# All gates of a five-branch encoder in the seven-product scheme, their sum in DRAM

## The chip, the cores and the metric

The kernel runs on one core of one Trainium2 chip. Times are device microseconds (us) of that core, from start to end of one execution; less is better. Engines: PE is TensorE, DVE is VectorE, ACT is ScalarE, POOL is GpSimd, and SP issues DMAs.

## What is computed (the reference, cut)

Two layers. In each, `h` is the normalised input of 1024 tokens by 1024 channels, five branches of 256 channels are computed from it, and each is projected to 1024 channels, gated and summed:

```python
for l in range(DEPTH):                                   # DEPTH = 2
    h = rmsnorm(x, norm_pre[l])
    (..., ca, cb, cz, ...) = split_cols(h @ w_in[l])
    y_cf = conformer_branch(ca, cb, cz, ...)             # and y_hg, y_sc, y_at, y_mem
    for n, yb in enumerate((y_hg, y_cf, y_sc, y_at, y_mem)):
        term = jax.nn.sigmoid(h @ w_gate[l, n]) * (yb @ w_branch[l, n])
        merged = term if merged is None else merged + term
    x = x + rmsnorm(merged @ w_out[l], norm_post[l])

def conformer_branch(a, b, z, ...):
    u = a * sigmoid(b)
    c = depthwise_conv(u, w_dw) + b_dw                   # 31 taps along the tokens
    mu = mean(c, channels); var = mean(square(c - mu), channels)
    n = (c - mu) * rsqrt(var + EPS) * ln_g + ln_b
    return silu(n) * silu(z)
```

## The kernel before, in words

Channels lie on the 128 partitions and tokens along the free axis, in halves of 512. Every fp32 product is made of three matmuls on values split into a high and a low part (`hi` made by a cast on ACT, `lo` by a subtraction on DVE), so a 128 x 128 weight block against 512 tokens is three matmuls of 128 x 512.

**Who sets the order.** `drive` (L465) runs a list of items, each a product with what is done to its result, and prepares the next item's weights while one runs. Work that is not a product (the convolution, attention, the forms below) is written as generators handed to `plan.side`; a planner with a small cost model puts pieces of them between the items. The order on each engine is thus fixed when the program is built, and every instruction carries the line of the planner's wrapper, L116.

**The gates.** `h @ w_gate` is five products of 1024 x 1024 per layer. Two forms exist. `gate_item` (L1137) is the plain one: 48 matmuls for 128 output channels. `strassen_items` (L1217) takes 256 output channels at a time, called a group, by seven products P1 to P7 of 12 matmuls instead of eight, 84 matmuls instead of 96. Their order is P1, P6, P5, P2, P7, P3, P4. P1 and P2 go to the PSUM bank `ps_gX`, P5 and P3 to `ps_gZ`, and P6, P7 and P4 to `ps_gY`. So P4 starts on `ps_gY` only when DVE has read P7's sum from it (`g_u<-ps_gY`, the `u3` of the code), and P7 only when DVE has read P6's. Beside it DVE adds and splits weight blocks (`g_s`, `raw_g`, `lo`) for products to come. The right-hand sides T1 to T4 are sums of blocks of `h`, made by `gate_forms` (L1175) on DVE: 32 additions `b<-h,h` that put high and low part together, further ones, and the splits.

**Before the change**, in each layer, branch 2 (eight items), the first quarter of branch 0 (two items) and the conformer's output gate `cz` (two items, `use_z`, L684) are plain; the other 15 groups are in the seven-product form, channel group by channel group, and each gated term is added by DVE to a running sum `mg` in SBUF (`merge`, L1261). The convolution and LayerNorm of the conformer (`conv`, L623) run on DVE and ACT beside the branch products (`ps_b`, 96 matmuls per branch) and the plain gates; two short matmul pairs, `cf_mu` and `cf_var`, make the means. The forms follow them.

Of the kernel before, what the change touches and what calls it, by code (L numbers as in the profile page):

```python
# [14 lines left out]
AF = mybir.ActivationFunctionType  # L15
# [5 lines left out]
P = 128  # L21
# [54 lines left out]
class Meter:  # L76
# [5 lines left out]
    def __getattr__(self, name):  # L82
        f = getattr(self.engine, name)

        def call(*args, **kw):
# [6 lines left out]
            if self.key == "PE":  # L92
                split = name != "transpose" and kw["rhs"].dtype == F32R
                if name == "transpose":
                    cost = 0.107
                elif split:
                    cost = 0.0135 + 0.000418 * n
                else:
                    tiled = outs[0].shape[0] <= HD or kw["lhsT"].shape[0] <= HD
                    cost = max(0.212, 0.00167 * n) * (0.7 if tiled else 1.0)  # L100
                cost += 0.09 * (split != self.plan.split)
                self.plan.split = split
            elif self.key == "DVE":
                n = max([n] + [prod(x.shape[1:]) for x in tiles])
                each = {"reciprocal": 0.0063, "tensor_scalar": 0.0005, "tensor_copy": 0.0006}.get(name, 0.00107)
                fixed = {"scalar_tensor_tensor": 0.16, "tensor_scalar": 0.23, "copy_predicated": 0.12}.get(name, 0.07)
                cost = fixed + n * each + 0.1 * ("accum_out" in kw)
            elif self.key == "ACT":
                cost = 0.055 + n * 0.00087 + 0.22 * ("accum_out" in kw) + self.plan.table(kw.get("func"))
            elif self.key == "DMA":  # L110
# [10 lines left out]
class Planner:  # L121


    def __init__(self):
        self.t = dict.fromkeys(("PE", "DVE", "ACT", "POOL", "DMA"), 0.0)
        self.written, self.read = {}, {}
        self.last = 0.0
        self.flags = set()
        self.sides = []
        self.rings = {}  # L130
        self.loaded = None
        self.split = True

    def add(self, key, cost, outs, ins):
# [3 lines left out]
        for x in outs:  # L138
            t = max([t] + [v for k, v in self.read.get(x, {}).items() if k != key])
        if key == "DMA":  # L140
            t = max(t, self.t["PE"])
        end = t + cost
        self.t[key] = end
        seen = end + (2.0 if key == "DMA" else 0.2)
        for x in outs:
# [66 lines left out]
def encoder(ctx: ExitStack, tc: tile.TileContext, a: dict, out: bass.AP):  # L212
# [5 lines left out]
    pool = Meter(nc.gpsimd, "POOL", plan)  # L218
    load = Meter(nc.sync, "DMA", plan).dma_start
    x_in = a["x"][0]  # L220
    mem_in = a["mem"][0]
# [389 lines left out]
    def conformer_items(l, hT, cs):  # L611
# [11 lines left out]
        def conv():  # L623
            yield f"merge{l}"
            for j in range(2):
                yield f"cf_u{l}{j}"
                u = us[j]
                c = cs[j] = slot(f"cf_c{j}")
                mid = CONFK // 2
                dve.tensor_scalar(out=c, in0=u, scalar1=wt[:, j, mid:mid + 1], scalar2=vec[:, j, 0:1],  # L630
                                  op0=ALU.mult, op1=ALU.add)
                for k in range(CONFK):
                    if k == mid:
                        continue
                    o = k - mid
                    dst = c[:, max(0, -o):T - max(0, o)]
                    src = u[:, max(0, o):T - max(0, -o)]
                    dve.scalar_tensor_tensor(out=dst, in0=src, scalar=wt[:, j, k:k + 1], in1=dst,
                                             op0=ALU.mult, op1=ALU.add)
                    if k % 2:  # L640
                        yield
            for s in range(2):
# [164 lines left out]
    def memory_attention_items(l, hT, kv, zs):  # L807
        qs = [None] * NH
        ks = []

        def stack_keys():
            for v in range(2):
                ks.append(slot(f"m_k{v}", F32R).rearrange("p (h m) -> p h m", h=NH))
                for h in range(NH):
                    rows = slice((h % 2) * HD, (h % 2 + 1) * HD)
                    for part in range(2):
                        act.copy(out=ks[v][part * HD:(part + 1) * HD, h, :],
                                 in_=kv["k"][rows, part ^ v, h // 2, :].bitcast(F32))

        items = []  # L820
        for j in range(2):
            def use_q(s, ps, j=j):
                if s == 0 and j == 0:
                    stack_keys()
                for hh in range(2):
# [6 lines left out]
        sc = HD ** -0.5  # L832

        def worker(j, par):
            yield f"m_in{l}{j}"
            for b in range(par, NT, 2):
# [35 lines left out]

        def workers():
            for j in range(2):
                for par in range(2):
# [299 lines left out]
    def gate_forms(l, hT, forms):  # L1175
# [15 lines left out]

        yield f"cf{l}"
        for i in range(2):
            if i:
                yield f"plain{l}"
            dst = {}
            for k in range(2):
                b11, b12, b22, b21 = (h2(f"b{x}") for x in range(4))
                for b, K, s in ((b12, 0, 1), (b11, 0, 0), (b22, 1, 1), (b21, 1, 0)):
                    hi, lo = (hT[s][v][2 * K + i][:, k, :].bitcast(F32) for v in range(2))  # L1200
                    dve.tensor_tensor(out=b, in0=hi, in1=lo, op=ALU.add)
                yield
                dve.tensor_tensor(out=b11, in0=b12, in1=b11, op=ALU.subtract)
# [13 lines left out]
    def strassen_items(l, groups, forms, pbd, mg, mgd, mT):  # L1217


        order = ("P1", "P6", "P5", "P2", "P7", "P3", "P4")  # L1220
        right = {"P1": "B11", "P2": "B21", "P3": "B22", "P4": "T4", "P5": "T1", "P6": "T2", "P7": "T3"}
# [4 lines left out]
        def load_group(gi):  # L1226
            n, g = groups[gi]
            wg = a["w_gate"][l, n].rearrange("(k p) c -> p k c", p=P)
            raws[gi] = []
            for d in (2 * g, 2 * g + 1):  # L1230
                raw = wp.tile([P, KC, P], F32, tag="raw", bufs=4, name=f"raw_g{n}{d}")
                load(out=raw, in_=wg[:, :, d * P:(d + 1) * P])
                raws[gi].append(raw)
# [48 lines left out]
        def after(k):  # L1282
            gi, name = k // N, order[k % N]
            n, g = groups[gi]
            b = banks[gi]
            if name == "P1":
                b["E1"] = h2("g_e1")
                act.copy(out=b["E1"], in_=b["X"])
                flush()
                if g not in mg:  # L1290
                    mg[g] = []
# [4 lines left out]
                pbs[gi] = []  # L1296
                for dd in range(2):
                    pbs[gi].append(slot("pb"))
# [26 lines left out]
            if gi == len(groups) - 1:  # L1325
                if name in ("P1", "P6", "P5"):
# [15 lines left out]
        for k in range(N * len(groups)):  # L1342
# [26 lines left out]

            need = f"forms{l}" if k == 1 else None  # L1370
            items.append(Item(prep, body, need))
# [60 lines left out]
    with tc.manual_schedule(engines={mybir.EngineType.PE, mybir.EngineType.DVE, mybir.EngineType.Activation,  # L1432
# [30 lines left out]
        def program():  # L1463
# [22 lines left out]
            for l in range(NL):  # L1486
# [8 lines left out]
                else:  # L1495
# [12 lines left out]
                mg = {0: [None, None]}  # L1508
                sc_g = [gate_item(l, 2, d, hT, pbd[2], mg[0], mgd[d // 2] if d > 1 else None, True)
                        for d in range(KC)]  # L1510
                hg_g = [gate_item(l, 0, d, hT, pbd[0], mg[0], None, False) for d in range(2)]
# [4 lines left out]
                cz[1].flag = f"plain{l}"  # L1516
                sc_b = branch_items(l, 2, y_sc, pbd[2])
                sc_b[0].flag = f"merge{l}"
                yield from sc_b
# [49 lines left out]
```

## Time and profile before

| What | Value |
|---|---|
| three runs | 2289.66, 2289.63, 2287.46 us; median 2289.63 |
| the profiled execution | 2287.26 us, of which the span shown is 2285.5 us |
| granted clock of PE, mean | 0.997 of full speed |
| busy in the span | PE 98%, PEld (weight loads) 81%, DVE 70%, ACT 43%, POOL 1% |
| stage of the 15 seven-product groups, layer 0 | 773.1 to 1058.7 us |
| the chain that ended last | PE 89%, DVE 7%, ACT 3% |

The busy share of PE counts its matmuls, not its waits; which waits end last in a stage is read from the timeline of that stage. Names in the trace are the program's without buffer numbers.

### The profile page before, as it was taken

To read this page: it belongs to the slowest core of one execution; us is meant where nothing else is said; L and a number is where in the kernel's file an instruction comes from. 1 tells how busy PE (TensorE), PEld (TensorE's weight loads), DVE (VectorE), ACT (ScalarE), POOL (GpSimd) and SP (SyncE) were. 2 spreads that over 40 slices of the span, in tenths; PEclk is the share of its full clock that TensorE was granted. 3 is DMA by queue.
4 is the path that set the end of the run, shared out by engine and by line. 5 is a ranking of instruction groups with operands and counts; after the bars stand their busy time and mean duration, and the time that the engine had idled before them with its cause. 6 is when DMAs were issued, how large, how long until landed. Compare 5 with 4: busy or idle time off the path is not lost.

```text
span 2285.5 us, 30510 instructions
## 1 busy us (share of the span) xinstructions
PE 2244.6 (98%) x11560; PEld 1841.1 (81%) x11560; DVE 1601.1 (70%) x2798; ACT 974.3 (43%) x1948; POOL 28.5 (1%) x41
## 2 busy tenths in 40 slices
PE   7999999999999999999999999999999999999998
PEld 6886788888888888887887878888788888888876
DVE  6768745347978688887667686363588696888865
ACT  5342435355435533335452423453453454333342
POOL 1000000000000000000110000000000000000000
PEclk9999999999999999999999999999999999999999
DMA  6102121103542633345440101211045535333244
GB/s 204 48 15 74 29 54 45 38 19 132 192 152 97 212 129 129 111 129 185 164 122 29 38 29 37 37 46 46 33 165 176 161 102 194 129 129 114 96 150 166
DMA packets 248019, 237.35 MB, mean 104 GB/s; under 512 B 29984, under 2 KB 191008, under 8 KB 247872
## 3 DMA queue, kind: packets, MB, share of 16 engines
q1 hardware_dynamic: 247872, 235.40, 31.7%
q8 instruction: 91, 1.49, 0.3%
q14 instruction: 56, 0.46, 0.1%
HBM read 177.69 MB, written 57.67 MB: 103 GB/s over the span
## 4 chain that ended last, share of the span: by engine, by line
PE 89%; DVE 7%; ACT 3%; issue 1%; DMA 0%; SPq 0%; POOL 0%; DVEq 0%; ACTq 0%; POOLq 0%
PE ps_gY L116 10%; PE ps_b L116 10%; PE ps_g L116 10%; PE ps_gX L116 7%; PE ps_o L116 7%; PE ps_gZ L116 7%; PE ps_hf L116 4%; PE h_s L116 2%; PE ps_cb L116 2%; PE ps_ca L116 2%; PE ps_at_z L116 2%; PE ps_hq L116 2%; PE ps_sz L116 2%; PE ps_cz L116 2%; PE ps_hz L116 2%; PE ps_sc L116 2%
## 5 line engine op out<-in xcount | busy, mean ns | idle before, releaser
L116 DVE TENSOR_TENSOR lo<-raw_g,hi 128x512 fp32r<-128x512 f32 x220 | 149.6, 688 | 91.7 <-ACT hi L116 91.5
L116 DVE SCALAR_TENSOR_TENSOR cf_c<-cf_u,cfw,cf_c 128x1009 f32<-128x1009 f32 (+14 forms) x120 | 153.1, 1276 | 3.0
L116 ACT CAST hi<-raw_g 128x512 fp32r<-128x512 f32 x220 | 133.4, 616 | 49.2 <-PE ps_gY L116 46.3
L116 PE MATMUL ps_b<-yh,hi 128*128 128x512 f32 x320 | 126.9, 397 | 0.0
L116 PE MATMUL ps_b<-yh,lo 128*128 128x512 f32 x320 | 124.7, 390 | 0.0
L116 PE MATMUL ps_b<-yl,hi 128*128 128x512 f32 x320 | 124.7, 390 | 0.0
L116 ACT COPY pb_out<-ps_b 128x512 f32<-128x512 f32 x160 | 91.7, 591 | 71.4 <-PE ps_b L116 59.6
L116 DVE TENSOR_TENSOR lo<-raw_in,hi 128x512 fp32r<-128x512 f32 x120 | 77.3, 686 | 40.6 <-ACT hi L116 40.4
L116 ACT ACTIVATE g_e<-g_e 128x512 f32<-128x512 f32 x60 | 38.0, 634 | 134.8 <-DVE g_e L116 134.8
L116 PE MATMUL ps_gX<-h_0h,hi 128*128 128x512 f32 x240 | 93.4, 389 | 0.0
L116 PE MATMUL ps_gX<-h_0h,lo 128*128 128x512 f32 x240 | 93.4, 389 | 0.0
L116 PE MATMUL ps_gX<-h_0l,hi 128*128 128x512 f32 x240 | 93.4, 389 | 0.0
L116 ACT CAST hi<-raw_in 128x512 fp32r<-128x512 f32 x120 | 69.2, 621 | 44.9 <-issue 18.7
L116 PEld LDWEIGHTS h_s<-hQQ,hkp 64*128 64x128 f32 x896 | 60.0, 187 | 21.7 <-issue 14.3
L116 PE MATMUL h_s<-hQQ,hkp 64*128 64x128 f32 x896 | 72.6, 294 | 2.8 <-ACT hkp L116 2.0
L116 DVE TENSOR_TENSOR lo<-raw_wo,hi 128x512 fp32r<-128x512 f32 x64 | 42.2, 688 | 47.2 <-PE ps_o L116 29.9
L116 DVE COPY_PREDICATED hS<-masks,h_s 128x512 f32<-128x512 uint8 x112 | 75.2, 726 | 0.0
L116 PEld LDWEIGHTS ps_b<-yh,hi 128*128 128x128 f32 x320 | 60.1, 188 | 13.3 <-issue 2.1
L116 PEld LDWEIGHTS ps_b<-yl,hi 128*128 128x128 f32 x320 | 60.1, 188 | 12.7
L116 ACT COPY hkp<-hK 128x512 f32<-128x512 f32 x56 | 37.3, 665 | 77.3 <-DVE hK L116 77.3
L116 PEld LDWEIGHTS ps_b<-yh,lo 128*128 128x128 f32 x320 | 60.2, 188 | 11.2
L116 ACT CAST hi<-raw_wo 128x512 fp32r<-128x512 f32 x64 | 37.8, 620 | 60.0 <-PE ps_o L116 47.0
(555 smaller groups left out, 6483.5 us busy)
## 6 DMA issues: line engine op xcount, KB each, us to landing
raw_g<-in_w_gate_dram SPq DMA_DIRECT2D x80, 512.0 KB, 3.5
pb<-pb_out SPq DMA_DIRECT2D x160, 256.0 KB, 2.5
pb<-pb SPq DMA_DIRECT2D x80, 512.0 KB, 4.6
raw_in<-in_w_in_dram SPq DMA_DIRECT2D x68, 512.0 KB, 3.7
raw_wo<-in_w_out_dram SPq DMA_DIRECT2D x32, 512.0 KB, 4.7
raw_b<-in_w_branch_dram SPq DMA_DIRECT2D x20, 512.0 KB, 4.9
mg<-g_th SPq DMA_DIRECT2D x24, 256.0 KB, 2.1
mg<-mg SPq DMA_DIRECT2D x12, 512.0 KB, 5.7
```

The source lines that it names most:

```text
L116: return f(*args, **kw)
```

## The change

1. All 20 gate groups of a layer take the seven-product form, branch by branch: `round1` has branches 2, 0, 3 and 4, and after the fifth branch product follow the four groups of branch 1. `gate_item` is no longer called. A seventeenth group in `round1`, named `z`, at index 15, computes `cz` in the same form.
2. In `round1` DVE only multiplies gate and branch (`merge`). Branch 2's terms are stored to DRAM (`mgd`) by SP; those of 0, 3 and 4 are added there by accumulating DMAs that POOL issues, 48 per layer. Branch 1's groups load that sum and go on as before.
3. In `gate_forms` the `b` additions become a copy DMA of the high part (SP) and an accumulating DMA of the low part (POOL), 16 per layer.
4. The convolution is split in token halves (240 instructions of up to 512 columns in place of 120 of about 1,015), waits for the flag `at{l}` instead of `merge{l}`, and its LayerNorm falls into the groups of `round1`. The memory branch's items stand earlier in the list, and its keys are stacked by a side generator on ACT.

Over both layers PE has 144 matmuls of 128 x 512 less: 960 of plain gates and 192 of `cz` go, and 12 groups of 84 come.

```diff
         def conv():
-            yield f"merge{l}"
+            yield f"at{l}"
...
-                dve.tensor_scalar(out=c, in0=u, scalar1=wt[:, j, mid:mid + 1], scalar2=vec[:, j, 0:1],
-                                  op0=ALU.mult, op1=ALU.add)
+                for s in range(2):
+                    dve.tensor_scalar(out=c[:, hs(s)], in0=u[:, hs(s)], ...)
+                yield
...
+                    for s in range(2):
+                        a, b = max(s * HALF, -o), min((s + 1) * HALF, T - max(0, o))
+                        dst, src = c[:, a:b], u[:, a + o:b + o]
+                        dve.scalar_tensor_tensor(out=dst, in0=src, scalar=wt[:, j, k:k + 1], in1=dst,
+                                                 op0=ALU.mult, op1=ALU.add)
+                    yield
...
                     hi, lo = (hT[s][v][2 * K + i][:, k, :].bitcast(F32) for v in range(2))
-                    dve.tensor_tensor(out=b, in0=hi, in1=lo, op=ALU.add)
-                yield
+                    load(out=b, in_=hi)
+                    accumulate(out=b, in_=lo)
+                yield f"plain{l}" if i else None
...
         def merge(gi, dd, s, th):
             n, g = groups[gi]
-            m, pb = mg[g][s][:, dd, :], pbs[gi][dd]
+            pb = pbs[gi][dd]
             dve.scalar_tensor_tensor(out=th, in0=th, scalar=1.0, in1=pb[:, hs(s)], op0=ALU.add, op1=ALU.mult)
-            dve.tensor_tensor(out=m, in0=m, in1=th, op=ALU.add)
+            if mT is not None:
+                m = mg[g][s][:, dd, :]
+                dve.tensor_tensor(out=m, in0=m, in1=th, op=ALU.add)
+            elif n == 2:
+                load(out=mgd[g][s][:, dd, :], in_=th)
+            else:
+                accumulate(out=mgd[g][s][:, dd, :], in_=th)
...
-                yield from cf
...
-                yield from hz + mem
...
-                yield from sc_g[:1] + branch_items(l, 0, o_hg, pbd[0]) + sc_g[1:3] + at_b + sc_g[3:] + hg_g
-                yield from cz + mem_b + branch_items(l, 1, y_cf, pbd[1])
-                groups = [(n, g) for g in range(4) for n in ((3, 4, 1) if g == 0 else (0, 3, 4, 1))]
-                yield from strassen_items(l, groups, forms, pbd, mg, mgd, mT)
+                hg_b = branch_items(l, 0, o_hg, pbd[0])
+                at_b[1].flag = f"plain{l}"
+                yield from mem[:2] + cf[:2] + mem[2:] + cf[2:] + hz + sc_b + hg_b + at_b + mem_b
+                round1 = [(n, g) for n in (2, 0, 3, 4) for g in range(4)]
+                round1.insert(15, ("z", C_CZ, y_cf, f"cf{l}", 0.25))
+                yield from strassen_items(l, round1, forms, pbd, None, mgd, None)
+                yield from branch_items(l, 1, y_cf, pbd[1])
+                yield from strassen_items(l, [(1, g) for g in range(4)], forms, pbd, {}, mgd, mT)
```

**The order on DVE around the reciprocal of the LayerNorm's first half, layer 0** (`cf_rs` is 1/sqrt of the variance; `lo`, `raw_g`, `g_s` prepare weights; `g_th` is a gate; `pb` a branch product). Before:

```order
L116 SCALAR_TENSOR_TENSOR g_th<-g_th,pb 128x512
L116 TENSOR_TENSOR lo<-raw_g_5821,hi 128x512 x2
L116 TENSOR_SCALAR cf_rs<-cf_var 128x512
L116 RECIPROCAL cf_rs<-cf_rs 128x512
L116 SCALAR_TENSOR_TENSOR g_th<-g_th,pb 128x512 x2
L116 TENSOR_TENSOR lo<-raw_g_5912,hi 128x512 x2
```

and now:

```order
L118 TENSOR_TENSOR g_u_6661<-ps_gY,g_e_6636 128x512
L118 TENSOR_TENSOR lo<-raw_g_6426,hi 128x512
L118 TENSOR_SCALAR cf_rs<-cf_var 128x512
L118 RECIPROCAL cf_rs<-cf_rs 128x512
L118 TENSOR_TENSOR lo<-raw_g_6428,hi 128x512
L118 TENSOR_TENSOR g_s_6709<-raw_g_6600 128x512
L118 TENSOR_TENSOR raw_g_6600<-raw_g_6598,raw_g_6600 128x512
L118 TENSOR_TENSOR lo<-raw_g_6598,hi 128x512
L118 TENSOR_TENSOR raw_g_6598<-g_s_6709,raw_g_6598 128x512
L118 TENSOR_TENSOR g_u_6727<-ps_gY,g_e_6636 128x512
```

The reciprocal stood between instructions of plain gates; it now stands inside a seven-product group, between the reads of P6's bank (first row) and of P7's (last row), with five weight instructions behind it.

**The order on POOL, layer 0, after the memory tokens' norm.** Before:

```order
L116 TENSOR_TENSOR rs_m_0_519<-ms_m_0_517,mhalf 128x1
L116 TENSOR_TENSOR rs_m_1_526<-ms_m_1_524,mhalf 128x1
L116 TENSOR_TENSOR rs_m_0_9249<-ms_m_0_9247,mhalf 128x1
L116 TENSOR_TENSOR rs_m_1_9256<-ms_m_1_9254,mhalf 128x1
L116 TENSOR_TENSOR rs_o_9529<-ms_o_9527,mhalf 128x1
```

and now:

```order
L118 TENSOR_TENSOR rs_m_1_526<-ms_m_1_524,mhalf 128x1
L118 DMA b_4786<-h_1l_261 128x512
L118 DMA b_4785<-h_0l_110 128x512
...
L118 DMA b_5673<-h_0l_113 128x512
L118 DMA mg_2985<-g_th 128x512
L118 DMA mg_2986<-g_e_6514 128x512
L118 DMA mg_2986<-g_u_6489 128x512
L118 DMA mg_2985<-g_e_6464 128x512
L118 DMA mg_2987<-g_th 128x512
```

POOL had nothing between the two layers' memory norms; it now issues 16 accumulating DMAs into `b` and then four per group into `mg`, each behind the instruction that makes its source and, for one place of `mg`, behind the store or accumulation before it.

## Rows read from the trace of the kernel before

**Rows 1.** The page of the profile: the span, part 1 (busy time and share of each engine), the granted clock of TensorE in 40 slices (part 2, in tenths), and the first row of part 4 (shares of the chain that ended last).
```profile
span 2285.5 us, 30510 instructions
...
PE 2244.6 (98%) x11560; PEld 1841.1 (81%) x11560; DVE 1601.1 (70%) x2798; ACT 974.3 (43%) x1948; POOL 28.5 (1%) x41
...
PEclk9999999999999999999999999999999999999999
...
PE 89%; DVE 7%; ACT 3%; issue 1%; DMA 0%; SPq 0%; POOL 0%; DVEq 0%; ACTq 0%; POOLq 0%
```

**Rows 2.** TensorE's waits over the whole span, longest sum first: what it waited for, us in total, times, longest. The first of fourteen rows; none of the fourteen names a tile of the gates or of the branches.
```profile
PE psT_x L116 <- DVE h_x L116: 8.7, 2, 7.9
```

**Rows 3.** Busy time by stretch: us of the stretch, its length, then busy us and (instructions) of PE, PEld, DVE, ACT and POOL, mean granted clock, DMA share, GB/s. The first stretch is layer 0's 15 seven-product groups from their first matmul to their last (1,260 matmuls; the count takes in the two that overlap its edges), the second lies in the output stage that follows them.
```profile
773.10:1058.70 285.60, 285.60 (x1262) 236.56 (x1261) 229.39 (x355) 113.27 (x198) 0.00 (x0) 1.00 0.39 131
...
1067.00:1071.00 4.00, 4.00 (x12) 3.10 (x12) 3.12 (x7) 3.73 (x6) 1.06 (x2) 0.57 0.54 159
```

**Rows 4.** Timeline of TensorE in one seven-product group of layer 0: start, duration, tile. The first row of P7, of P3, of P4, and of the next group's P7.
```profile
860.12 0.39 PE L116 MATMUL ps_gY<-T3h,hi 128*128 128x512 f32 x1
...
862.84 0.39 PE L116 MATMUL ps_gZ<-h_1h,hi 128*128 128x512 f32 x1
...
865.56 0.39 PE L116 MATMUL ps_gY<-T4h,hi 128*128 128x512 f32 x1
...
879.16 0.39 PE L116 MATMUL ps_gY<-T3h,hi 128*128 128x512 f32 x1
```

**Rows 5.** Timeline of VectorE in the same group: start, duration, tile, and in brackets the idle time before it and its releaser.
```profile
861.46 0.69 DVE L116 TENSOR_TENSOR lo<-raw_g,hi 128x512 fp32r<-128x512 f32 x1 [0.70 <-ACT hi L116]
...
863.04 0.69 DVE L116 TENSOR_TENSOR g_u<-ps_gY,g_e 128x512 f32<-128x512 f32 x1 [0.16 <-PE ps_gY L116]
863.76 0.69 DVE L116 TENSOR_TENSOR g_e<-g_u,g_e 128x512 f32<-128x512 f32 x1
...
865.09 0.69 DVE L116 TENSOR_TENSOR mg<-mg,g_th 128x512 f32<-128x512 f32 x1
865.70 0.68 DVE L116 TENSOR_TENSOR lo<-raw_g,hi 128x512 fp32r<-128x512 f32 x1
866.30 0.68 DVE L116 TENSOR_TENSOR g_u<-ps_gZ,g_u 128x512 f32<-128x512 f32 x1
...
877.77 0.69 DVE L116 TENSOR_TENSOR lo<-raw_g,hi 128x512 fp32r<-128x512 f32 x1 [2.47 <-ACT hi L116]
```

**Rows 6.** Timeline of VectorE in layer 0's gate stage where the LayerNorm's first half runs today.
```profile
666.97 0.69 DVE L116 TENSOR_SCALAR cf_rs<-cf_var 128x512 f32<-128x512 f32 x1 [1.27 <-PE cf_var L116]
668.36 3.35 DVE L116 RECIPROCAL cf_rs<-cf_rs 128x512 f32<-128x512 f32 x1 [0.70 <-ACT cf_rs L116]
671.63 0.63 DVE L116 SCALAR_TENSOR_TENSOR g_th<-g_th,pb 128x512 f32<-128x512 f32 x1
...
676.89 0.68 DVE L116 TENSOR_TENSOR cf_c<-cf_c,cf_rs 128x512 f32<-128x512 f32 x1
678.52 0.55 DVE L116 TENSOR_SCALAR cf_c<-cf_c,cfv 128x512 f32<-128x512 f32 x1 [0.95 <-ACT cf_t L116]
...
681.93 0.69 DVE L116 SCALAR_TENSOR_TENSOR cf_c<-cf_t,cf_c 128x512 f32<-128x512 f32 x1
```

**Rows 7.** Timeline of ScalarE in the same place.
```profile
656.57 0.62 ACT L116 CAST cf_muh<-cf_sum 128x512 fp32r<-128x512 f32 x1 [3.11 <-DVE cf_sum L116]
...
660.44 1.23 ACT L116 ACTIVATE cf_sq<-cf_c 128x512 f32<-128x512 f32 x2 [2.62 <-DMA mg<-g_th]
662.43 0.62 ACT L116 CAST cf_varh<-cf_sq 128x512 fp32r<-128x512 f32 x1 [0.76 <-DVE cf_sq L116]
...
664.81 1.28 ACT L116 ACT_TABLE_LOAD   x1
667.70 0.63 ACT L116 ACTIVATE cf_rs<-cf_rs 128x512 f32<-128x512 f32 x1 [1.60 <-DVE cf_rs L116]
```

**Rows 8.** Timeline of TensorE in the output stage that follows the gates of layer 0: a first wait, a second, and matmuls of the slower level.
```profile
1065.24 0.50 PE L116 MATMUL ps_o<-hi,mT0h 128*128 128x512 f32 x1 [0.96 <-ACT hi L116]
1065.58 0.39 PE L116 MATMUL ps_o<-hi,mT0l 128*128 128x512 f32 x1
1066.78 0.50 PE L116 MATMUL ps_o<-lo,mT0h 128*128 128x512 f32 x1 [0.81 <-DVE lo L116]
...
1067.50 0.63 PE L116 MATMUL ps_o<-hi,mT0l 128*128 128x512 f32 x1
```

**Rows 9.** Groups of instructions on VectorE (busy us, mean ns, idle before): the convolution, the `mg` additions of one kind, the additions of the forms.
```profile
L116 DVE SCALAR_TENSOR_TENSOR cf_c<-cf_u,cfw,cf_c 128x1009 f32<-128x1009 f32 (+14 forms) x120 | 153.1, 1276 | 3.0
...
L116 DVE TENSOR_TENSOR mg<-mg,g_e 128x512 f32<-128x512 f32 x60 | 41.5, 692 | 2.1
...
L116 DVE TENSOR_TENSOR b<-b,b 128x512 f32<-128x512 f32 x32 | 22.1, 690 | 0.8
```

**Rows 10.** Groups of instructions on GpSimd, the costliest of three with work (41 instructions in all), and DMA issues (KB each, median us from issue to landing; all on SP's queue).
```profile
L116 POOL TENSOR_TENSOR rs_x<-ms_x,mhalf 128x1 f32<-128x1 f32 x16 | 15.4, 965 | 28.5 <-DVE ms_x L116 28.4
...
raw_g<-in_w_gate_dram SPq DMA_DIRECT2D x80, 512.0 KB, 3.5
pb<-pb_out SPq DMA_DIRECT2D x160, 256.0 KB, 2.5
...
mg<-g_th SPq DMA_DIRECT2D x24, 256.0 KB, 2.1
```

More of the change, by code (lines that the diff above doesn't have):

```diff
@@ L1 @@
 from contextlib import ExitStack
-from functools import cache
+from functools import cache, partial
 from math import prod
@@ L109, in call @@
                 cost = 0.055 + n * 0.00087 + 0.22 * ("accum_out" in kw) + self.plan.table(kw.get("func"))
+            elif self.key == "SWDMA":
+                cost = 1.2
             elif self.key == "DMA":
@@ L124, in __init__ @@
     def __init__(self):
-        self.t = dict.fromkeys(("PE", "DVE", "ACT", "POOL", "DMA"), 0.0)
+        self.t = dict.fromkeys(("PE", "DVE", "ACT", "POOL", "DMA", "SWDMA"), 0.0)
         self.written, self.read = {}, {}
@@ L139, in add @@
             t = max([t] + [v for k, v in self.read.get(x, {}).items() if k != key])
-        if key == "DMA":
+        if key in ("DMA", "SWDMA"):
             t = max(t, self.t["PE"])
@@ L143, in add @@
         self.t[key] = end
-        seen = end + (2.0 if key == "DMA" else 0.2)
+        seen = end + (2.0 if key in ("DMA", "SWDMA") else 0.2)
         for x in outs:
@@ L629, in conv @@
                 mid = CONFK // 2
-                dve.tensor_scalar(out=c, in0=u, scalar1=wt[:, j, mid:mid + 1], scalar2=vec[:, j, 0:1],
-                                  op0=ALU.mult, op1=ALU.add)
+                for s in range(2):
+                    dve.tensor_scalar(out=c[:, hs(s)], in0=u[:, hs(s)], scalar1=wt[:, j, mid:mid + 1],
+                                      scalar2=vec[:, j, 0:1], op0=ALU.mult, op1=ALU.add)
+                yield
                 for k in range(CONFK):
@@ L811, in stack_keys @@
         def stack_keys():
+            yield f"at{l}10"
             for v in range(2):
                 ks.append(slot(f"m_k{v}", F32R).rearrange("p (h m) -> p h m", h=NH))
-                for h in range(NH):
-                    rows = slice((h % 2) * HD, (h % 2 + 1) * HD)
+            for h in range(NH):
+                rows = slice((h % 2) * HD, (h % 2 + 1) * HD)
+                for v in range(2):
                     for part in range(2):
@@ L832, in memory_attention_items @@
         sc = HD ** -0.5
+        plan.side(stack_keys(), idle="ACT")
         def worker(j, par):
+            yield f"m_k{l}"
             yield f"m_in{l}{j}"
@@ L873, in workers @@
         def workers():
+            yield f"m_in{l}0"
             for j in range(2):
@@ L1190, in put @@
                 forms[f"T{x}"][v].append(dst[x][v][:, k, :])
-        yield f"cf{l}"
+        yield f"mem{l}"
         for i in range(2):
-            if i:
-                yield f"plain{l}"
             dst = {}
@@ L1226, in load_group @@
         def load_group(gi):
-            n, g = groups[gi]
-            wg = a["w_gate"][l, n].rearrange("(k p) c -> p k c", p=P)
+            n, g = groups[gi][:2]
+            zs = n == "z"
+            wg = (a["w_in"][l] if zs else a["w_gate"][l, n]).rearrange("(k p) c -> p k c", p=P)
             raws[gi] = []
-            for d in (2 * g, 2 * g + 1):
+            for d in (0, P) if zs else (2 * g * P, (2 * g + 1) * P):
                 raw = wp.tile([P, KC, P], F32, tag="raw", bufs=4, name=f"raw_g{n}{d}")
-                load(out=raw, in_=wg[:, :, d * P:(d + 1) * P])
+                at = g + d if zs else d
+                load(out=raw, in_=wg[:, :, at:at + P])
                 raws[gi].append(raw)
@@ L1262, in merge, with times @@
             n, g = groups[gi]
-            m, pb = mg[g][s][:, dd, :], pbs[gi][dd]
+            pb = pbs[gi][dd]
             dve.scalar_tensor_tensor(out=th, in0=th, scalar=1.0, in1=pb[:, hs(s)], op0=ALU.add, op1=ALU.mult)
-            dve.tensor_tensor(out=m, in0=m, in1=th, op=ALU.add)
-        def gate(gi, dd, s, th, src=None):
+            if mT is not None:
[5 more added lines that the diff above has]
+                accumulate(out=mgd[g][s][:, dd, :], in_=th)
+        def gate(gi, dd, s, th, src=None):
+            if groups[gi][0] == "z":
+                y, z = groups[gi][2][dd][:, hs(s)], th if src is None else src
+                if src is None:
+                    th = h2("g_tz")
+                act.activation(out=th, in_=z, func=AF.Tanh, scale=0.5)
+                def times():
+                    dve.scalar_tensor_tensor(out=th, in0=th, scalar=1.0, in1=z, op0=ALU.add, op1=ALU.mult)
+                    dve.scalar_tensor_tensor(out=y, in0=y, scalar=groups[gi][4], in1=th, op0=ALU.mult, op1=ALU.mult)
+                late.append(times)
+                return
             act.activation(out=th, in_=th if src is None else src, func=AF.Tanh, scale=0.5)
@@ L1283, in after @@
             gi, name = k // N, order[k % N]
-            n, g = groups[gi]
+            n, g = groups[gi][:2]
+            zs = n == "z"
             b = banks[gi]
@@ L1289, in after @@
                 flush()
-                if g not in mg:
+                if mT is not None and g not in mg:
                     mg[g] = []
@@ L1296, in after @@
                 pbs[gi] = []
-                for dd in range(2):
+                for dd in range(0 if zs else 2):
                     pbs[gi].append(slot("pb"))
@@ L1324, in after @@
                 gate(gi, 1, 0, b["E1"])
-            if gi == len(groups) - 1:
+            if mT is None and name == "P4" and gi == len(groups) - 1:
+                flush()
+            if mT is not None and gi == len(groups) - 1:
                 if name in ("P1", "P6", "P5"):
@@ L1368, in body @@
                 yield
-            need = f"forms{l}" if k == 1 else None
+            need = f"forms{l}" if k == 1 else groups[k // N][3] if groups[k // N][0] == "z" and k % N == 0 else None
             items.append(Item(prep, body, need))
@@ L1507, in program @@
                 mgd = [[dram.tile([P, 2, HALF], F32, name=f"mg{l}{g}{s}") for s in range(2)] for g in range(4)]
[L1508 to L1511, printed above, removed]
                 forms = {}
```

14 lines of the change are left out of this document (3 added, 11 removed).

## The prediction, made before the changed kernel ran

> **What bounds the kernel now.** Read the page first. TensorE is busy 2244.6 of 2285.5 us, the chain that ended last is PE for 89%, and its granted clock is full in every slice [rows 1]. A busy share alone doesn't say that matmuls are what each stage waits for, so the waits come next: the largest sum is 8.7 us for the norm's `h_x`, and no row names a gate or a branch [rows 2]. In the window of the 15 seven-product groups 1,260 matmuls take 285.60 us with PE busy throughout [rows 3], 226.7 ns each; the timeline says the same, since from one group's P7 to the next group's are 19.04 us for 84 matmuls [rows 4]. So in the stage that the change enlarges nothing but the number of matmuls counts, as long as DVE and ACT keep up. DVE is the one to watch. It is busy 229.39 of those 285.60 us [rows 3], and in one group idles only 0.70, 0.16 and 2.47 us [rows 5].
>
> **The change part by part.** The sum is made against the profiled execution, 2287.3 us (span 2285.5 and 1.8 around it). The three runs' median lies 2.4 above it and the lowest run 0.2.
>
> *Matmuls.* 144 fewer by 226.7 ns [rows 3] is **-32.6 us**. All of it is on the path, because PE doesn't wait there now.
>
> *Additions on DVE.* 96 additions into `mg` go, at 0.692 us or 0.61 of DVE's pitch (865.09 to 865.70) [rows 5, 9], and 32 `b` additions at 0.69 [rows 9]. The convolution pays some of it back: 240 instructions of at most 512 columns, like the 0.68 to 0.69 us of other 512-column instructions [rows 5], against 120 at 1.276 [rows 9], about +12 us. All of that is beside PE: it counts only where DVE is late. Adding up DVE's instructions at these durations per stage of the new order, the branch products hold 19 to 21 us of DVE work per 21.7 us of PE (96 matmuls), the first group of `round1` 21.4 per 19.0, the others 13.7 to 17.9. DVE isn't the bound on average, except in that first group.
>
> *The first group.* It starts with eight halves of the convolution and the last of the forms still on DVE, and T2 is wanted by its P6. Its excess is 21.4 - 19.0 = 2.4 us; at least none of it (DVE was ahead) and at most all of it shows. I take 0.8 per layer: **+1.6** (0 to 4.8).
>
> *The LayerNorm inside the groups.* This is the main loss. Before, the chain of `cf_rs` runs beside plain gates, whose banks nobody needs soon. Now it stands between DVE's two reads of `ps_gY`, as the order shows, and P4 can't start before the second of them, `g_u<-ps_gY` after P7. In the group of rows 4 and 5 that read starts at 863.04 and P4 at 865.56, so 1.8 us are spare after its 0.69 [rows 4, 5].
>  - Reciprocal group. Count from the end of P5, which `cf_var` follows. P4 is due after P2, P7 and P3, 2.72 us each [rows 4], and two `cf` matmuls: 8.6. ACT first copies `ps_gZ` (about 0.6), loads a table 1.28 and takes the root 0.63 [rows 7]; the reciprocal holds DVE 3.27 (668.36 to 671.63) [rows 6]; five weight instructions of 0.60 to 0.72 pitch [rows 5] make 3.2; the read 0.69; handing over between engines some 0.3. That is 10.0, **1.4 late**. In the trace of before the table load was done early and DVE waited only 0.70 for the root [rows 6, 7]; now the copy stands ahead of it on ACT.
>  - Mean group. `cf_mu` comes two thirds into P2, so about 2.7; two subtractions 1.3; the second square and its wait 0.8, the addition 0.69, then `cf_varh` 0.62 (its DVE input 0.76 earlier) and `cf_varl` 0.69 [rows 6, 7]; the same five and the read. That ends at about 10.1 against 8.6: **1.45 late**.
>  - Tanh group. From 676.89 to 682.62 its six DVE instructions and two waits for `cf_t` took 5.7 us [rows 6]; with ACT's copy in front they end at 5.4, and five and the read at 9.3 against 8.2: **1.1 late**.
>
>  Three groups by two halves by two layers: 4 x 3.95 = **+15.8**. Lowest 0 (if DVE starts these chains with the spare 1.8 us in hand), highest 4 x 3 x 2.5 = 30.
>
> *The clock.* A late P4 makes PE stand. In the output stage a wait of 0.96 us was followed by full speed, a second one of 0.81 just after it by matmuls every 0.43 us instead of 0.23 [rows 8], with a granted clock of 0.57 (the 1.2 GHz level for most of it) [rows 3]: ten such matmuls, 1.7 us more. The same pair in layer 1 cost none. Twelve stalls of 1.1 to 1.45 us lie between those cases; I take two drops, **+3.4** (0 to 20).
>
> *Accumulating DMAs.* No row shows one. From below, a plain store of the same 256 KB lands in 2.1 us; from above, a POOL instruction of 1.0, a 512 KB load's 3.5 and that store's 2.1 in a row, 6.6 [rows 10]. I take the middle, about 4, as the descriptor work is new and the bytes few. Who waits, counted in the new order at the pace of [rows 4, 5]: a buffer of a gated term is rewritten 7.5 to 8.4 us after its DMA is issued in the LayerNorm groups (once 5.9, by ACT's square), over 14 us in the others; the same place of `mg` comes again after 36 us or more; a `b` is read 7.7 us or later. So up to about 7 us costs **0** (below 5.9 no reader waits at all). The Trainium skill, page "DMA: Bandwidth & Descriptors", section "Anatomy of one DMA", gives about 2.0 us plus bytes over 436 GB/s for a DMA that GpSimd issues, by it an estimate of 2.6 us and the same 0; no run here shows it yet.
>
> *The rest.* SP gets 44 issues more on 594, each landing in some 2.1 to 3.5 us [rows 10] and prefetched by a group; the memory attention mixes with window attention earlier, and branch products wait at a few places for casts. No row prices this. The waits of before are the nearest thing, one sum of 8.7 us and thirteen smaller ones [rows 2]; I take **+3**, a third of the largest (-3 to 8.7).
>
> Sum: -32.6 + 1.6 + 15.8 + 3.4 + 3 = -8.8, that is 2278.5 by the profiled execution. Up to 2.4 above it lies the median, so I forecast **2279 us**.
>
> **The rivals.**
> 1. *No new stalls.* If the chains start early enough, only the matmuls and the small rest remain: -32.6 + 1 to 5, 2256 to 2260. For it: DVE has 1 to 5 us spare per group. Against: in-order DVE can't use idle time that lies behind a wait for ACT.
> 2. *The clock falls at every stall.* 12 x 1.7 = 20 in place of 3.4: 2295, within or just above no change. For it: two rows of waits shorter than these [rows 8]. Against: layer 1's pair.
> 3. *Accumulations land late (slower).* If one takes 12 us, each of the 12 LayerNorm groups waits 12 - 8 = 4 us, in all 48: 2279 + 48 = 2327. From 15 us on the other 18 groups wait as well. It decides the sign from about 9.5 us on. For it: POOL has never issued a DMA here, and its 128x1 instruction takes 0.965 us beside the first norms, where DVE works too [rows 10]. Against: only four 256 KB transfers per group of 19 us, while the queue in use fills under half of the engines [rows 3]. The Trainium skill has a rule that speaks for this rival: page "SBUF — State Buffer", the box on the "DVE blocks DMA" trap, says that GpSimd can't write a DMA's descriptors while DVE runs an operation in a mode with two ports (fp32 copies, and tensor_scalar by its section "Who interferes with whom"), though tensor_tensor has no such mode. By that rule the delay here is small: the tensor_scalar rows last 0.55 and 0.69 us [rows 6], and nearly all of DVE's work in the groups is tensor_tensor.
> 4. *DVE lags.* The convolution's halves don't fit beside the branches and delay forms and first groups by more than 2.4 us each: 2285 to 2295.
> That the change doesn't do what it says is excluded for the matmuls, since the new order holds 144 fewer.
>
> **How the numbers follow.** About 4.6 us (0.2%) is what a measurement can tell from no change. Forecast (2268 to 2285): 0.45. Rival 1: 0.18. Rival 2 and rival 4, 2285 to 2300: 0.22, most of it under 2294.2. Rival 3: 0.15. So faster 0.64, same 0.16, slower 0.20. The range of 8 in 10 leaves out the far ends of rivals 1 and 3: **2257 to 2304**.
>
> **What would show it.** Right: in the groups with `cf_rs`, `cf_mu` and `cf_t`, PE rows of `ps_gY<-T4h` waiting for DVE `g_u` by 1 to 1.5 us, none in other groups; 19.04 us for a plain group; `mg` accumulations landing in 2 to 6.6 us with nobody waiting for them. Wrong: waits for DMA `mg` or `b`, a stage of the groups with a lower granted clock, PE waiting for T2 for several us, or no wait of PE at all. The forecast falls if stalls in all come to under 10 or over 32.6 us.

## The result: 1% slower, with the matmuls saved and two stages that wait

The changed kernel takes 2312.15 us (median of four runs, 2311.17 to 2312.92) against 2288.55 for the kernel before on the same chip, a ratio of 1.0103 with a 95% interval of 1.0086 to 1.0121. The forecast was 2279 us, faster than before; the time lies above the upper end of its range, 2304.

The page of the profile after, its span, busy times and chain, to be held against [rows 1]:

```profile
span 2309.9 us, 31029 instructions
...
PE 2226.2 (96%) x11416; PEld 1817.3 (79%) x11416; DVE 1622.7 (70%) x2938; ACT 1006.7 (44%) x2008; POOL 140.3 (6%) x169
...
PE 82%; DVE 9%; issue 3%; ACT 3%; DMA 2%; SPq 0%; DVEq 0%; ACTq 0%; POOL 0%
```

The span grew by 24.4 us. PE is busy 18.4 us less, not 32.6, and its idle time grew from 40.9 to 83.7. Where it idles stands in its waits (what for, us in total, times, longest), of which [rows 2] had none in gates or branches:

```profile
PE ps_b L118 <- ACT pb_out L118: 20.8, 6, 6.8
PE ps_gY L118 <- DVE g_u L118: 17.8, 13, 2.2
...
PE ps_b L118 <- ACT hi L118: 2.3, 2, 1.1
PE ps_b L118 <- DVE lo L118: 2.1, 2, 1.0
```

The two largest are new, and they lie in two stages. The windows of layer 0 after (columns as in [rows 3]) are the four branch products in a row, `round1`, branch 1 and its four groups; the last row shows the matmul with which branch 1 begins:

```profile
531.30:633.70 102.40, 90.65 (x385) 73.83 (x385) 77.99 (x115) 55.72 (x98) 10.71 (x12) 0.95 0.85 266
633.70:974.20 340.50, 330.63 (x1438) 271.00 (x1436) 256.84 (x390) 142.12 (x245) 39.83 (x46) 0.99 0.62 151
974.20:997.40 23.20, 22.16 (x97) 18.11 (x98) 8.62 (x13) 11.56 (x21) 1.76 (x2) 1.00 0.79 236
997.40:1073.50 76.10, 76.10 (x337) 63.04 (x336) 59.52 (x90) 32.20 (x55) 0.00 (x0) 1.00 0.57 200
```

```profile
974.17 0.50 PE L118 MATMUL ps_b<-yh,hi 128*128 128x512 f32 x1 [1.13 <-ACT hi L118]
```

Now set each beside its matmuls at 226.7 ns [rows 3]. The branch products, 384 matmuls, should take 87.0 us and take 102.4; `round1`, 1,436 with the `cf` pairs, should take 325.5 and takes 340.5; branch 1, 96, 21.8 and takes 23.2; the last four groups, 336, 76.2 and take 76.1. So 15.4 + 15.0 + 1.4 us are lost in layer 0, and by the same reading 12.9 + 12.7 + 1.4 in layer 1 (its windows: 99.9, 338.2, 23.2 us). That is 58.8 us against the 32.6 saved, 26.2 net; the output stage of layer 0, which this time kept its full clock, gives 1.6 back. The attention stages before the branch products lost nothing. The edges hide one thing: branch 1's first wait (the last row) ends where its window begins, so 1.3 us per layer that stand with `round1` belong to branch 1, which lost 2.7 us in each layer.

**In the groups** the stalls are those foretold. PE's rows of the reciprocal group, then ACT's and DVE's (rows of before: [rows 6, 7]):

```profile
740.88 0.39 PE L118 MATMUL cf_var<-cf_varh,mean_w 128*128 128x512 f32 x1
...
751.00 0.47 PE L118 MATMUL ps_gY<-T4h,hi 128*128 128x512 f32 x1 [1.34 <-DVE g_u L118]
```

```profile
741.13 0.59 ACT L118 COPY g_e<-ps_gZ 128x512 f32<-128x512 f32 x1 [2.11 <-PE ps_gZ L118]
741.74 1.28 ACT L118 ACT_TABLE_LOAD   x1
743.03 0.63 ACT L118 ACTIVATE cf_rs<-cf_rs 128x512 f32<-128x512 f32 x1
```

```profile
741.53 0.69 DVE L118 TENSOR_SCALAR cf_rs<-cf_var 128x512 f32<-128x512 f32 x1 [1.02 <-PE cf_var L118]
743.70 3.35 DVE L118 RECIPROCAL cf_rs<-cf_rs 128x512 f32<-128x512 f32 x1 [1.47 <-ACT cf_rs L118]
746.97 0.63 DVE L118 TENSOR_TENSOR lo<-raw_g,hi 128x512 fp32r<-128x512 f32 x1
...
750.17 0.68 DVE L118 TENSOR_TENSOR g_u<-ps_gY,g_e 128x512 f32<-128x512 f32 x1
```

ACT's copy of `ps_gZ` (end of P5) begins at 741.13, the root is done at 743.66, the reciprocal at 746.97, and the read of `ps_gY` for which P4 waits ends at 750.85. That is 9.7 us after the copy began and 10.0 after `cf_var` took over from P5 (the first row), where the working had 10.0. The waits of layer 0 are 1.38, 1.34, 1.26 and, for the second half, 2.16, 1.34, 1.25 us, in the order mean, reciprocal, tanh; layer 1's agree within 0.01. What the page calls idle leaves out the 0.16 by which a matmul's modelled end outlasts its pitch, and the matmul after it starts 0.08 late, so each stall costs 0.2 to 0.3 more. After the longest the clock fell (PE's rows and a window):

```profile
793.46 0.54 PE L118 MATMUL ps_gY<-T4h,hi 128*128 128x512 f32 x1 [2.16 <-DVE g_u L118]
...
794.22 0.63 PE L118 MATMUL ps_gY<-T4l,hi 128*128 128x512 f32 x1
...
797.41 0.40 PE L118 MATMUL ps_gY<-T4h,lo 128*128 128x512 f32 x1
```

```profile
793.80:797.00 3.20, 3.20 (x9) 2.52 (x8) 2.60 (x5) 1.57 (x3) 0.86 (x1) 0.50 0.26 25
```

From 793.79 to 796.78 matmuls start every 0.43 us, at a granted clock of 0.50 (the 1.2 GHz level), and then every 0.23 again. Of the twelve stalls of both layers only this one was followed by such a stretch; it cost 1.6 us.

**In the branch products** ACT and PE stand still together. ACT, PE, POOL and the window (columns as in [rows 3]):

```profile
617.86 1.56 ACT L118 COPY pb_out<-ps_b 128x512 f32<-128x512 f32 x3
630.34 0.59 ACT L118 COPY pb_out<-ps_b 128x512 f32<-128x512 f32 x1 [10.93 <-DMA pb<-pb_out]
```

```profile
630.98 0.79 PE L118 MATMUL ps_b<-yh,hi 128*128 128x512 f32 x1 [6.80 <-ACT pb_out L118]
```

```profile
616.14 0.87 POOL L118 DMA_DIRECT2D b<-h_1l  x1 [44.44 <-DMA b<-h_0h]
...
617.86 1.85 POOL L118 DMA_DIRECT2D b<-h_0l  x1
```

```profile
616.00:632.00 16.00, 9.20 (x40) 7.26 (x38) 10.01 (x15) 3.48 (x7) 3.57 (x4) 0.83 0.94 238
```

ACT's copy out of `ps_b` waits 10.93 us for a store of an earlier `pb_out` to land (its buffers come from a ring of eight, `h2` in the code, that `b` shares), and PE, whose four banks are then full, waits 6.80. Around 616 us one step of the forms issues four copies and four accumulations, beside two 512 KB weight loads and the branch stores; the 16 DMA engines are busy 0.94 of this window. Each layer has three such bursts in these products, and one of its three waits for `pb_out` follows each. The DMA lists give the issues with KB and median us to landing; then come the stores' landing (min/median/max) before, the same after, that of layer 0's three bursts of accumulations, and the queues after (packets, MB, share of 16 engines), to be held against [rows 10]:

```profile
pb<-pb_out SPq DMA_DIRECT2D x160, 256.0 KB, 2.9
...
mg<-g_e POOLq DMA_DIRECT2D x48, 256.0 KB, 4.1
...
b<-h_1h SPq DMA_DIRECT2D x16, 256.0 KB, 2.3
...
b<-h_1l POOLq DMA_DIRECT2D x16, 256.0 KB, 5.6
b<-h_0l POOLq DMA_DIRECT2D x16, 256.0 KB, 7.6
```

```profile
DMA to landing us min/median/max: 2.0/2.5/6.9
```

```profile
DMA to landing us min/median/max: 2.0/2.9/11.8
```

```profile
DMA to landing us min/median/max: 4.7/8.2/12.6
```

```profile
q1 hardware_dynamic: 254208, 247.98, 32.8%
q0 software_dynamic: 18432, 33.56, 10.1%
```

The store's median went from 2.5 to 2.9 us, its longest from 6.9 to 11.8. The accumulations into `b` outside the bursts, eight in all, landed in 3.4 to 4.6 us; the medians of the list, 5.6 and 7.6, mix both kinds. An accumulation of 256 KB takes 10.1% x 2309.9 / 128 = 1.82 us of all 16 engines on average; the other queue moves as many bytes in 0.80.

### The profile page after: what moved, and what is told of

Read it like the earlier page. It is cut to its first block, busy times and chain, and to the rows that moved or that the text cites. A ratio compares the mean times of both kernels' runs of the same rounds, so it can differ in the third digit from the quotient of the medians.

```text
span 2309.9 us, 31029 instructions
## 1 busy us (share of the span) xinstructions
PE 2226.2 (96%) x11416; PEld 1817.3 (79%) x11416; DVE 1622.7 (70%) x2938; ACT 1006.7 (44%) x2008; POOL 140.3 (6%) x169
## 3 DMA queue, kind: packets, MB, share of 16 engines
q0 software_dynamic: 18432, 33.56, 10.1%
## 4 chain that ended last, share of the span: by engine, by line
PE 82%; DVE 9%; issue 3%; ACT 3%; DMA 2%; SPq 0%; DVEq 0%; ACTq 0%; POOL 0%
PE ps_gY L118 13%; PE ps_gX L118 9%; PE ps_gZ L118 8%; PE ps_b L118 8%; PE ps_o L118 7%; PE ps_hf L118 4%; PE h_s L118 2%; PE ps_mq L118 2%; PE ps_m_z L118 2%; PE ps_cb L118 2%; PE ps_ca L118 2%; PE ps_at_z L118 2%; PE ps_hz L118 2%; PE ps_sz L118 2%; PE ps_hq L118 2%
## 5 line engine op out<-in xcount | busy, mean ns | idle before, releaser
L118 DVE TENSOR_TENSOR lo<-raw_g,hi 128x512 fp32r<-128x512 f32 x240 | 165.0, 688 | 106.2 <-ACT hi L118 106.1
L118 ACT CAST hi<-raw_g 128x512 fp32r<-128x512 f32 x240 | 147.4, 614 | 54.8 <-PE ps_gY L118 48.7
L118 DVE SCALAR_TENSOR_TENSOR cf_c<-cf_u,cfw,cf_c 128x512 f32<-128x512 f32 (+8 forms) x240 | 163.9, 741 | 0.0
L118 PE MATMUL ps_b<-yh,hi 128*128 128x512 f32 x320 | 127.8, 399 | 23.1 <-ACT pb_out L118 20.8
L118 PE MATMUL ps_gX<-h_0h,hi 128*128 128x512 f32 x336 | 131.6, 392 | 0.0
L118 PE MATMUL ps_gX<-h_0h,lo 128*128 128x512 f32 x336 | 131.4, 391 | 0.0
L118 PE MATMUL ps_gX<-h_0l,hi 128*128 128x512 f32 x336 | 131.2, 391 | 0.0
L118 POOL DMA_DIRECT2D b<-h_1l x16 | 17.9, 1120 | 1108.1 <-DVE cf_c L118 973.8
L118 PE MATMUL ps_gY<-T4h,hi 128*128 128x512 f32 x168 | 67.1, 399 | 17.8 <-DVE g_u L118 17.8
L118 DVE TENSOR_TENSOR g_u<-ps_gY,g_e 128x512 f32<-128x512 f32 x84 | 57.7, 687 | 25.1 <-PE ps_gY L118 25.1
L118 PEld LDWEIGHTS ps_gX<-h_0h,lo 128*128 128x128 f32 x336 | 63.6, 189 | 13.4
```

Source lines behind the costliest of these rows:

```text
L118: return f(*args, **kw)
```

## The experiments

Theory A: there are two separate losses, the forms' DMAs crowding the DMA engines beside the branch stores, and LayerNorm chains too long for a group. Ten kernels test it; the ratio is to the kernel before, run beside each.

| Run | Median us | Ratio (95%) |
|---|---|---|
| the change | 2312.15 | 1.0103 (1.0086 to 1.0121) |
| b_by_dve | 2280.12 | 0.9968 (0.9957 to 0.9980) |
| b_copy_only | 2286.05 | 0.9990 (0.9980 to 0.9999) |
| ln_spread | 2294.24 | 1.0025 (1.0015 to 1.0034) |
| mg_plain_store | 2311.50 | 1.0103 (1.0086 to 1.0120) |
| spread_and_dve | 2266.02 | 0.9895 (0.9879 to 0.9912) |
| spread_and_pool | 2284.27 | 0.9977 (0.9968 to 0.9986) |
| b_eighth | 2293.91 | 1.0016 (1.0007 to 1.0025) |
| b_apart | 2369.95 | 1.0352 (1.0336 to 1.0367) |
| split_early | 2261.10 | 0.9879 (0.9863 to 0.9896) |
| conv_whole | 2270.92 | 0.9919 (0.9904 to 0.9933) |

**b_by_dve.**

```diff
-                    load(out=b, in_=hi)
-                    accumulate(out=b, in_=lo)
+                    dve.tensor_tensor(out=b, in0=hi, in1=lo, op=ALU.add)
```

> The sums b of the forms are made by VectorE again (32 additions), all else as in the change. Theory A (the form DMAs fill the 16 DMA engines just when the branch products are stored, the stores land late, ACT's pb_out waits for its buffer and TensorE for ps_b): the ps_b waits for pb_out fall from 20.8 us to under 3, the clock lost behind them (about 7 us) comes back, so 2312 - 18 - 7 = about 2287. Rival B (the branch stage is late because VectorE and ScalarE are late in program order there): 32 x 0.61 = 20 us more for VectorE in a stage with no room, the waits stay above 15 us and the time is 2312 or more.

32 us faster than the change. The waits for `pb_out` are gone from the list, the branch stages take 87.0 us in both layers, and the stores land in 5.6 us at most (PE's wait in the groups, and the stores' landing):

```profile
PE ps_gY L118 <- DVE g_u L118: 14.7, 10, 2.2
```

```profile
DMA to landing us min/median/max: 2.0/2.3/5.6
```

Theory A holds and B falls, although DVE has more to do. The gain is larger than the two stages' excess of 28.3. About 2 us more are the slower matmuls at the head of `round1`, which follow the last wait for `pb_out`, and the groups have 10 waits in place of 13. The rest is not settled: this kernel's executions lie between 2278.7 and 2286.2 us, and the profiled one is the slowest of them.

**b_copy_only.** The line with `accumulate` is dropped.

> The copies of the high parts into b stay on SP, the accumulating DMAs of the low parts are left out (so the forms lack the low parts). Theory A: an accumulating DMA takes 1.8 us of all 16 engines (10.1% of the span for 128 of them), a copy of the same size 0.8, so most of the crowding goes: waits for pb_out 6 us or less, time 2286 to 2295. If the copies on SP's queue are the cause, the waits stay at 15 us or more and the time at 2305 or more.

Without the low parts in the forms the kernel takes 2286.05 us, with 0.8 us of waits for `pb_out` and 87.7 and 88.0 us for the branch stages: not the copies but the accumulations do it.

**b_eighth.**

```diff
-                    accumulate(out=b, in_=lo)
+                    accumulate(out=b[:, :64], in_=lo[:, :64])
```

> The accumulating DMAs into b stay in number and place but add 64 of the 512 columns only (the forms lack most of the low parts). Theory A (bytes on the DMA engines): the waits for pb_out fall below 5 us, 2284 to 2292. Rival R (what costs is the fixed time of an accumulating DMA, during which the b buffers stay occupied in the ring of eight that pb_out shares): 12 us or more of waits remain, 2300 or more.

```profile
PE ps_b L118 <- ACT pb_out L118: 5.5, 4, 2.0
```

```profile
b<-h_1l POOLq DMA_DIRECT2D x16, 32.0 KB, 4.1
b<-h_0l POOLq DMA_DIRECT2D x16, 32.0 KB, 5.1
```

This kernel leaves out most of the low parts. 5.5 us of 20.8 remain, just above A's 5, and 2293.91 lies above A's 2292 and below R's 2300. So most of it goes with the bytes. About a quarter of the waits remains, which fits a fixed time (32 KB still need 4.1 and 5.1 us to land), though no run shows that cause alone.

**b_apart.** A `yield` after each copy and each accumulation.

> The four pairs of copy and accumulation per step are issued one after the other, with a turn of the planner after each copy and each accumulation, instead of together; bytes and number are the change's. Theory A (a burst of the four, with weight loads and branch stores, is more than the DMA engines move in time): waits for pb_out under 10 us, 2285 to 2300. Rival R (the b buffers are held too long in the ring): they are held longer here, so 20 us or more and 2312 or more.

The waits for `pb_out` are gone, the branch stages take 87.0 us and the accumulations land in 3.6 and 3.3 us (medians). So R falls, by which these waits should have grown. That it was the burst and not the number is not shown: of the twelve accumulations that each layer had in this stage, six now come behind it. And A missed the time by 70 us. PE's longest waits:

```profile
PE cf_mu L118 <- ACT cf_muh L118: 54.0, 4, 18.5
PE ps_gY L118 <- ACT T2h L118: 21.3, 2, 10.7
PE cf_var L118 <- ACT cf_varh L118: 14.0, 4, 3.5
```

Forms that take more turns are late for P6 of the first group. There `drive` waits for their flag and runs the side generators meanwhile, so the whole LayerNorm lands ahead of the forms in the order, with PE idle (in layer 0 `cf_mu` first runs at 632 us, and P6 of the first group, after its wait for T2, at 678).

**ln_spread.** Three more `yield`s per half: after the squares, between the root and the reciprocal, and after each of the two tanh instead of after both.

```diff
                     act.activation(out=sq[j], in_=c, func=AF.Square)
+                yield
...
                 act.activation(out=rs, in_=rs, func=AF.Sqrt)
+                yield
                 dve.reciprocal(out=rs, in_=rs)
...
-                yield
+                    yield
```

> The LayerNorm's generator hands back to the planner three more times per half (after the squares, before the reciprocal, after each tanh), so its pieces fall into twice as many groups; same arithmetic. Theory A (each stall is a LayerNorm chain too long for one group): the ps_gY waits for g_u fall from 17.8 us to under 3 and the clock behind them (about 9 us) comes back: 2285 to 2292. Rival C (VectorE is short of time in these groups whatever the order): the same 15 us or more of waits, in more and shorter pieces, 2308 to 2314.

```profile
PE ps_b L118 <- ACT pb_out L118: 18.8, 6, 6.3
...
PE ps_gY L118 <- DVE g_u L118: 1.9, 4, 0.6
```

17.8 us of waits became 1.9 with the same instructions, and the time fell by 18; the branch stage still waits. `round1` takes 329.2 us in place of 340.5. C falls; at 2294.24 the time is 2 us above A's range.

**mg_plain_store.** `merge` stores in place of accumulating for all of `round1`, so the sum over the branches is left out.

> The 96 accumulating DMAs into mg become plain stores by SP (so the sum over branches is not made). Theory A: nobody waits for them, the time stays within 3 us of 2312 and the waits in the groups stay at 17 to 18 us. Rival D (their traffic, twice that of a store, delays weight loads or the branch products' loads, or GpSimd's descriptor work holds VectorE up): over 5 us faster, with shorter waits in the groups after the fourth.

2311.50, with the same waits in the groups as the change, 17.8 us in 13 times: against plain stores the 96 accumulations into `mg` cost nothing that can be measured. D falls.

**spread_and_dve.** The two diffs of b_by_dve and ln_spread.

> Both mends together: the sums b on VectorE as before the change, and the LayerNorm handed back to the planner three more times per half. Theory A (the two losses are apart from each other): 2312 - 32 - 18 = 2262, within 4; waits for pb_out 0, for g_u under 3. Rival B2 (VectorE's 20 us of b additions push the convolution so far into the groups that the spread LayerNorm comes too late for the z group): 2270 or more, with waits in the groups with cf tiles.

2266.02, at the upper end of A's range. Its waits for `pb_out` are gone and those for `g_u` are 1.9 us. Together the two mends give 46 us, apart 32 and 18: the losses add up within 4 us.

**spread_and_pool.** In spread_and_dve, the sums `b` are made by `pool.tensor_tensor` in place of `dve.tensor_tensor`.

> As the one before, but the 32 sums b are made by GpSimd, which is idle there. If GpSimd's additions leave VectorE alone, VectorE has 20 us less work in the branch stage than with its own additions and the time is 2258 to 2264. If a 128x512 addition on GpSimd takes several us and slows VectorE's two-input instructions beside it, VectorE rows in the branch stage grow beyond 0.69 us and the time is 2268 or more.

Slower than with DVE by 18 us. PE's wait in the branch products, and DVE's, POOL's and ACT's rows of one stretch (start, duration, operation):

```profile
PE ps_b L118 <- ACT pb_out L118: 10.9, 6, 4.2
```

```profile
609.48 3.48 DVE L118 SCALAR_TENSOR_TENSOR cf_c<-cf_u,cfw,cf_c 128x512 f32<-128x512 f32 x2
```

```profile
610.67 1.74 POOL L118 TENSOR_TENSOR b<-h_0h,h_0l 128x512 f32<-128x512 f32 x1
612.37 1.74 POOL L118 TENSOR_TENSOR b<-h_1h,h_1l 128x512 f32<-128x512 f32 x1
```

```profile
620.55 0.62 ACT L118 CAST hi<-raw_g 128x512 fp32r<-128x512 f32 x1 [6.88 <-DVE raw_g L118]
```

Two convolution instructions take 1.74 us each (3.48 for both), the time of POOL's addition beside them, where the kernel after needs 0.68 on average (163.9 us for 240). VectorE's weight preparation behind them (`raw_g`) comes late and ACT waits 6.88 us for it, ahead of its copies out of `ps_b`; 10.9 us of PE's waits for `pb_out` return without one form DMA. The Trainium skill, page "SBUF — State Buffer", section "Who interferes with whom", has VectorE instructions with two SBUF inputs contend with GpSimd's reads; these rows agree.

**split_early.** In spread_and_dve, branch 1's high and low parts are made by a side generator (`act.copy`, `yield`, `dve.tensor_tensor`), started by a flag that the z group's last product sets; `put` uses them.

> Both mends as in spread_and_dve; in addition branch 1's input is split into its high and low parts by a side generator during the last group of round1 instead of at the start of branch 1. Theory: the waits there, 1.1 for the cast and 1.0 us for the lo of the weights in each layer, 4.4 us in all with about 1.5 of clock behind them, come from those splits standing ahead of the weights on ACT and VectorE; they fall below 1 us and the time to 2261 to 2264. Rival: the weights' own casts are late by the one-item lookahead, whatever stands ahead; the waits and 2266 stay.

```profile
span 2259.8 us, 30934 instructions
...
PE 2216.6 (98%) x11416; PEld 1816.9 (80%) x11416; DVE 1638.5 (73%) x2970; ACT 1005.9 (45%) x2008; POOL 111.6 (5%) x137
```

```profile
PE ps_gY L118 <- DVE g_u L118: 1.9, 4, 0.6
```

2261.10, and both waits at branch 1 are gone (21.8 us, no excess). This version beats both kernels: 27 us under the kernel before, of the 32.6 that the matmuls are worth.

**conv_whole.** In spread_and_dve, the convolution's instructions are whole again, as before the change.

> As spread_and_dve, with the convolution's instructions whole again (120 of about 1,015 columns at 1.28 us for 240 of 512 at 0.69). Theory: VectorE is not the bound in the branch stage once the sums b are its own, so 12 us less of its work gives nothing: 2264 to 2268. Rival E (longer instructions stand in the way of short ones that TensorE waits for): waits of TensorE for lo or T tiles in the branch stage, 2270 or more.

2270.92 against 2266.02, with intervals that overlap and profiled spans 0.6 us apart: unclear, though not faster. The time lies above the theory's 2268, in rival E's range, but E's waits for `lo` or T tiles in the branch stage are not there; waits of 0.4 us for `pb_out` in each layer are new. 11 us less of DVE's busy time (1638.5 to 1627.9) gave nothing.

## Why the prediction was wrong

- **Matmuls, -32.6.** Right. With the other terms mended, 27 us are kept (split_early); the last four groups run at 76.1 us for 336 matmuls.
- **Accumulating DMAs, 0. The step that failed.** It asked who reads a `b` or rewrites a buffer, and bounded one DMA's landing at 6.6 us by rows of loads and stores of the kernel before. In bursts of four they took 4.7 to 12.6 us (layer 0), so the bound was wrong as well. But the loss came from a place it had not asked about, namely who shares the 16 engines with them: the branch stores, for whose buffers ACT and then PE waited. The step cost 28.3 us by stages (15.4 + 12.9), about 30 with the slower matmuls that follow at the head of `round1`, and 32 by b_by_dve. Rival 3 named late accumulations, but put them in the LayerNorm groups (its turning point, 9.5 us, comes out at 8.9 by its own numbers: 8 and a twelfth of 2289.6 - 2279). For `mg` the step was right: medians of 3.8 to 4.2 us for the 4 taken, and nobody waiting. The Trainium skill has a rule by which VectorE's operations in a two-port mode keep GpSimd from writing descriptors (page "SBUF — State Buffer", the box on the "DVE blocks DMA" trap). No cost of it is seen here: POOL's 96 issues for `mg` take 0.87 us in the median and 1.20 at most. From the Trainium skill, page "DMA: Bandwidth & Descriptors", section "Anatomy of one DMA", the prediction had an estimate of 2.6 us; the trace has 3.8 to 4.2, and the measurement decides.
- **LayerNorm, +15.8.** The mechanism and the places were right: twelve stalls, at P4, behind `g_u`. The size was low: 17.4 us by PE's rows and 20.3 from matmul to matmul. The second half's mean group waits 2.16, since ACT does the copy of `ps_gZ` ahead of `cf_muh` there; the working had taken both halves alike. Its terms for the mean group, as listed, add up to 10.7 and not to 10.1, so the closeness of the first half's wait to the 1.45 is in part luck.
- **The clock, +3.4.** One of the twelve stalls was followed by a stretch of the slower level, for 1.6 us. Four more such stretches follow waits for `pb_out` and belong to the failed step. Rival 2 fell.
- **The first group, +1.6.** 0.9 us in both layers, with one wait of 0.38 us (layer 1). That wait was at P4 for `g_u` and not at P6 for T2, as the term had it.
- **The rest, +3.** 5.5 us were lost at branch 1, and the output stage of layer 0 gave 1.6 back. The term had named waits for casts, but not their cause: the split of branch 1's input stands ahead of its weights (split_early).
- These terms, -32.6 + 30.1 + 20.3 + 1.6 + 0.9 + 5.5 - 1.6, make 24.2 of the 24.4 us by which the span grew.
- Rival 1 fell with the twelve stalls. Of rival 4 nothing is seen but the 0.9 us of the first groups.
- Without the failed step the time would have lain in the range: b_by_dve, which undoes it alone, takes 2280.1 us. That it is within about 1 us of the 2279 forecast is partly luck: its executions spread over 7 us, and in the change itself the other terms were off by up to 4.5.

## What to carry to other kernels

Moving additions from an engine to DMAs moves them to a resource that others share too: add up the share of the DMA engines in that very stretch, where an accumulation cost about twice a copy here, and ask whose transfers come behind them. A chain through several engines that is put between two reads of one PSUM bank must fit the time between them; cut into pieces, the same instructions cost 1.9 us of waits here in place of 17.8. Where a planner waits for a flag, more turns for one generator can pull others in front of it (b_apart).

## What the runs showed of the hardware

An accumulating DMA of 256 KB took 1.82 us of all 16 engines on average, 2.3 times the other queue's 0.80 per 256 KB. Those from SBUF into SBUF alone took 1.5 us (mg_plain_store: 2.1% x 2308.1 / 32). Accumulations of 256 KB landed in 3.8 to 4.2 us into DRAM, one at a time (medians), and in 4.7 to 12.6 in bursts of four into SBUF beside other transfers (layer 0, median 8.2); those of 32 KB still needed 4.1 and 5.1 us (medians in b_eighth). A GpSimd addition of 128x512 (mean 1.58 us) stretched VectorE's two-input instructions beside it from 0.68 to 1.74 us. After single waits of 1.25 to 1.4 us in the groups the clock stayed at its upper level; after one of 2.16 us it stayed there in layer 1 and fell in layer 0.
